# Emitting the stores, squares and splits of finished residual blocks three row pairs later

## The chip, the cores and the metric

The kernel runs on one core of one Trainium2 chip. The metric is the device time of one execution in microseconds (us). The kernel before takes 2199.36 us, the median of three runs (2192.54 to 2201.11). All work of the core goes through five engines: TensorE (PE, matmuls into PSUM), VectorE (DVE), ScalarE (ACT), GpSimd (POOL), and SyncE (SP), which here issues every DMA.

## The reference, cut to what matters

The model has two layers over one sequence of 1024 tokens of width 1024. Layer 0 is an RG-LRU block, layer 1 a chunked band attention whose keys and values are computed once from the residual stream after layer 0. Each layer ends in the same MLP:

```
def sqrelu_mlp(x, w_up, w_down):
    return jnp.square(jax.nn.relu(x @ w_up)) @ w_down

for l in range(DEPTH):                      # DEPTH = 2
    h = h + recurrent_block(...)            # l = 0
    h = h + o @ b_w_o[j]                    # l = 1, after attention
    h = h + sqrelu_mlp(rmsnorm(h, mlp_norm[l]), w_up[l], w_down[l])
```

The hidden width is 4096. The change is in the product with `w_down` and in what follows it: the finished residual block of layer 0 is stored (attention adds to it later), squared (for the next RMS norm) and split (as an operand of the next projections); that of layer 1 is the output and is stored only.

## The kernel before, in words

**Numbers.** Activations are held transposed: 128 features on the partitions, half of the tokens (512 columns, `h` 0 or 1) in a tile. Every float32 product is done as three matmuls on fp32r operands (`mm`, lines 321 to 323): high part by high part, low weight by high part, and so on. So each weight block and each activation block has first to be split: ACT copies it to the high part, DVE subtracts that from the source to get the low part (`wsplit`, lines 732 and 733, for weights; `split`, lines 334 and 335, for activations).

**The down product.** `mlp_down` (line 805) is one level of a fast 2 by 2 block multiplication: instead of eight half-size products it does seven, in the order n = 0, 1, 5, 4, 6, 2, 3. Each product runs over 16 row pairs q of the hidden dimension. For a row pair, `block(n, q)` gets one weight block (loaded from HBM, or kept from an earlier product and added to), and splits it; `operand(n, q)` loads one activation block from the scratch tensor `hid` and splits it; then 12 matmuls (four PSUM banks, three each) use both. Products 0, 5, 6 and 3 accumulate in the banks `Z` (tags pj and sc), products 1, 4 and 2 in `Y` (tags tp and po), so that neighbours always use different banks.

**After a product**, `add` (line 851) adds the four banks to residual blocks `X[j][h]`, four DVE instructions. After products 1, 6 and 2 four blocks are complete, and `finish(j0, h)` (line 853) calls `done` for each. In layer 0 `done1` (line 912) stores the block to `x2d`, and `o2.last` squares it on ACT (line 368), adds the square to a running sum on DVE (line 374; not for the first block of a half, which begins the sum) and splits it (lines 334, 335). In layer 1 `done2` (line 1324) only stores it to the output. After product 3, the last one, the last four blocks are finished one by one.

**Buffers.** Landing buffers `raw`: 8. Pool `w` (16 tiles): split weights, and the split operands of products 0, 1, 5 and 4. Pool `g` (66 tiles): the residual blocks, weight sums kept between products, the running sum of squares, the split finished blocks, and the split operands of products 6, 2 and 3 (line 846: `where=gr if n in (6, 2, 3) else wr`). A row pair takes two tiles for the weight and two for the operand.

**What sets the order.** In this stage the order of instructions on an engine isn't written out by hand. A scheduler of the framework orders them when the program is built, on a model of the times, with the program's order as priority, and it hands out the tiles of the pools. Each engine then runs its list in order. (Attention is different: there the order is that in which the kernel's own planner emits it.) After product 2, `ahead()` (layer 0 only, `begin_later`, line 307) begins to load and prepare the weights of the attention stage.

Of the kernel before, what the change touches and what calls it, by code (L numbers as in the profile page):

```python
# [36 lines left out]
FR = 0.9  # L37
LAT = 0.3
C_DMA = 3.8
JP = 2  # L40
SC = (2.5, 5.0)
AHEAD = 1
# [111 lines left out]
def tile_yoco_rglru_chunk_attention(  # L154
# [30 lines left out]
    def nm(s):  # L185
        cnt[0] += 1
        return f"{s}_{cnt[0]}"

    def gf(s="g"):
        return gp.tile([P, H2], F32, tag="g", name=nm(s))  # L190
# [7 lines left out]
    def rawf():  # L198
        return wp.tile([P, H2], F32, tag="raw", name=nm("raw"), bufs=NRAW)
# [10 lines left out]
    def bank(tag=None):  # L210
        if tag is None:
            tag = ("pj", "tp", "sc", "pj", "tp", "sc", "po", "sc")[ring[0] % 8]
            ring[0] += 1
        return ps1.tile([P, H2], F32, tag=tag, name=nm(tag), bufs=BANKS[tag])

    def hs(h):
        return slice(h * H2, (h + 1) * H2)
# [3 lines left out]
    def dma(dst, src):  # L221
        ins = nc.sync.dma_start(dst, src)
        if early[0]:
            early[0] -= 1
            tc.keep_in_program_order(ins)
# [28 lines left out]
    for t in range(NF):  # L254
        later += [(w_kv[t], g_kv, pool), (w_q[t], g_q, pool), (w_kv[NF + t], g_kv, pool)]
    later += [(w_o[j], None, WOE) for j in range(JP)]
    later.append((w_o[:, :, NF - 1, :].rearrange("j p m -> p j m"), None, dve))
    later += [(w_o[j], None, dve) for j in range(JP, NF)]
    loading, ready = [], []
# [58 lines left out]
    def mm(ps, wp_, xp, start, stop, more=False):  # L318

        (wh, wl), (xh, xl) = wp_, xp  # L320
        pe.matmul(ps, lhsT=wh, rhs=xh, start=start, stop=False, skip_group_check=more)  # L321
        pe.matmul(ps, lhsT=wh, rhs=xl, start=False, stop=False, skip_group_check=more)  # L322
        pe.matmul(ps, lhsT=wl, rhs=xh, start=False, stop=stop, skip_group_check=more)  # L323

    def mm3(ps, w, xs, half, span=None):
        n = len(xs)
        for k in range(n) if span is None else span:
            mm(ps, wparts(w, k), xs[k][half], k == 0, k == n - 1)

    def split(src, gain=None, where=gr):  # L330
        h = where("h")
        l = where("l")
        if gain is None:
            act.activation(h, src, AF.Copy)  # L334
            dve.tensor_tensor(l, src, h.bitcast(F32), ALU.subtract)  # L335
        else:
            act.activation(h, src, AF.Copy, scale=gain)
            dve.scalar_tensor_tensor(l, src, gain, h.bitcast(F32), ALU.mult, ALU.subtract)  # L338
        return h, l
# [319 lines left out]
    class Out:  # L659
# [54 lines left out]

        def whole(self, Z, j0):
            ws = {}
            for j, h in out_order(j0):
                if j not in ws:
                    ws[j] = next_w()
                ps = bank()  # L720
                mm3(ps, ws[j], Z, h)
                self.first(ps, j, h)
                self.last(j, h)

    def wload(src):
        raw = rawf()
        dma(raw, src)
        return raw

    def wsplit(raw):  # L730
        wh, wl = wr("wh"), wr("wl")
        act.activation(wh, raw, AF.Copy)  # L732
        dve.tensor_tensor(wl, raw, wh.bitcast(F32), ALU.subtract)  # L733
        return blocks4(wh), blocks4(wl)
# [70 lines left out]
    def mlp_down(o, layer, done, ahead=None):  # L805
        X = [[gf("x") for _ in range(2)] for _ in range(NF)]
        S = [None] * NQ
        S2 = [None] * NQ

        def block(n, q):  # L810

            def load(x):
                return wload(w_down[layer, q, x])

            if n == 0:
                a11, a21 = load(A11), gf("s3")
                dma(a21, w_down[layer, q, A21])
                w = wsplit(a11)
                dve.tensor_tensor(a21, a21, a11, ALU.add)
                S[q] = a21  # L820
            elif n == 1:
                a12, a22 = load(A12), gf("s2")
                dma(a22, w_down[layer, q, A22])
                w = wsplit(a12)
                dve.tensor_tensor(a22, a22, S[q], ALU.add)
                S2[q] = a22
            elif n == 5:
                w = wsplit(S2[q])
                a12 = load(A12)
                dve.tensor_tensor(S2[q], S2[q], a12, ALU.add)  # L830
            elif n == 4:
                a21, a22 = load(A21), load(A22)
                dve.tensor_tensor(a21, a21, a22, ALU.add)
                w = wsplit(a21)
            elif n == 6:
                w = wsplit(S[q])
            elif n == 2:
                w = wsplit(S2[q])
            else:
                w = wsplit(load(A22))  # L840
            return w

        def operand(n, q):
            t = rawf()
            dma(t, hid[n, q])
            return split(t, where=gr if n in (6, 2, 3) else wr)

        def add(banks, j0, h, op):
            for x in range(4):
                xt = X[j0 + x][h]  # L850
                dve.tensor_tensor(xt, xt, banks[x], op)

        def finish(j0, h):
            for x in range(4):
                done(j0 + x, h, X[j0 + x][h])

        Z = [bank(tag) for tag in ("pj", "pj", "sc", "sc")]
        for n in (0, 1, 5, 4, 6, 2, 3):
            if n in (1, 4):
                Y = [bank(tag) for tag in ("tp", "tp", "tp", "po")]  # L860
            banks = Y if n in (1, 4, 2) else Z
            start = n in (0, 1, 4)
            held = []
            for q in range(NQ):
                held.append((block(n, q), operand(n, q)))
                if n == 0 and q < NF:
                    for h in range(2):
                        dma(X[q][h], o.keep[q, :, hs(h)])
                if n == 3 and NQ - 4 <= q < NQ - 1:
                    continue  # L870
                for x in range(4):
                    for p, ((wh, wl), t) in enumerate(held):
                        mm(
                            banks[x], (wh[:, x, :], wl[:, x, :]), t,
                            start and q == 0, q == NQ - 1 and p == len(held) - 1, not start,
                        )
                held = []
            if n == 0:
                add(Z, 0, 0, ALU.add)
            elif n == 1:  # L880
                add(Y, 0, 0, ALU.add)
                finish(0, 0)
            elif n == 5:
                add(Z, 0, 1, ALU.add)
            elif n == 4:
                add(Y, 4, 1, ALU.subtract)
            elif n == 6:
                add(Z, 4, 1, ALU.subtract)
                finish(4, 1)
            elif n == 2:  # L890
                add(Y, 0, 1, ALU.add)
                finish(0, 1)
                if ahead is not None:
                    ahead()
            else:
                for x in range(4):
                    xt = X[4 + x][0]
                    dve.tensor_tensor(xt, xt, Z[x], ALU.subtract)
                    done(4 + x, 0, xt)
# [16 lines left out]

    mlp_up(o1, 0)
    mlp_down(o1, 0, done1, begin_later)


# [13 lines left out]
    class Proj:  # L934
# [35 lines left out]
        def normed(self, kind, h, ps):  # L970
# [51 lines left out]
            for e, st in enumerate((even, odd)):  # L1022
                (self.K if keys else self.Q)[e][h] = st
            self.made[kind, h].set(plan.t + C_DMA)

# [51 lines left out]
    def load_bias(hd):  # L1077
        b = biases[hd] = sf(640)
        dma(b, relb[hd])
        yield plan.t + C_DMA  # L1080
        pool.tensor_scalar(b, b, -1.0, 1.0, ALU.mult, ALU.mult)
# [4 lines left out]
    class Unit:  # L1086
# [142 lines left out]
        def reload(self, k, h):  # L1229
            ot = sf()  # L1230
            dma(ot, od[k, :, hs(h)])
            yield plan.t + C_DMA
            yield from self.halves(k, h, ot, REL)
# [13 lines left out]
    def wo_steps():  # L1247
        for j0 in range(0, JP, 2):
            js = range(j0, min(j0 + 2, JP))
            ws = []  # L1250
# [17 lines left out]
    def filling():  # L1268
        for t in range(NF):
            projs.append(Proj(t))  # L1270
            n = 0
            for y in projs[t].steps():
                if y is None:
                    n += 1
                    if t == NF - 1 and 0 <= n - 5 * NF - 2 < NF - 2:
                        plan.start(units[0].reload(n - 5 * NF - 2, 0))
                yield y
        yield from wo_steps()

    fill = filling()  # L1280
    total = 8 * 6 * NF + 2 * JP * (NF - 1)
    cost = [1.0 if n.h else FR for n in units]
# [31 lines left out]
    wl7 = next_w()  # L1314
    for j in range(JP):
        for h in range(2):
# [71 lines left out]
```

## Time and profile before

| what | us |
|---|---|
| median of three runs | 2199.36 |
| profiled execution, its own time | 2197.24 |
| its span, first to last instruction | 2195.5 |
| TensorE busy in it | 2113.9 |
| VectorE busy | 1583.7 |
| ScalarE busy | 1115.1 |
| down products of layer 0, about | 655.9 to 985.2 |
| down products of layer 1, about | 1878.7 to 2191.3 |

The profile is one execution. Times in it run from its first instruction. Busy time of matmuls overlaps (each is shown 0.39 us long, but the next one starts 0.23 us after it), so progress of PE is read here from the starts of matmuls, and a loss from a start that comes later than the one before it allows.

### The profile page before, as it was taken

Reading aid. Unit: us, or ns where it says so; the run is one execution under the profiler, and the core shown is the slowest. Engines: PE = TensorE matmul, PEld = TensorE weight load, DVE = VectorE, ACT = ScalarE, POOL = GpSimd, SP = SyncE. Lnnn points to the kernel's source line nnn. Section 1 sums busy time; section 2 is a strip of 40 time slices with the busy share of each in tenths; the row PEclk is TensorE's granted clock in tenths of the full one; section 3 lists DMA queues with packets and bytes.
Section 4 is the critical chain, followed back from the end, with each engine's and each line's share of the span. In section 5 each row is a group of like instructions: output and inputs, shape, how many; then the busy total and the mean of one; then the engine's idle time right before and its main releaser. Section 6 shows DMA issues by size and latency. Waiting matters only on the chain.

```text
span 2195.5 us, 29616 instructions
## 1 busy us (share of the span) xinstructions
PE 2113.9 (96%) x9753; PEld 1741.9 (79%) x9753; DVE 1583.7 (72%) x2716; ACT 1115.1 (51%) x2030; POOL 659.8 (30%) x567
## 2 busy tenths in 40 slices
PE   7898898999999999998999999999999999999999
PEld 5676686888888888776888888878788888888887
DVE  7788867777777775554777777777677777777843
ACT  4576745443444544444666666675443443444632
POOL 5454311333320000105666656651223333000000
PEclk8999999999999999999999999999999999999999
DMA  5111144444459774343333333353354444977733
GB/s 178 37 48 37 37 141 134 163 149 149 154 196 328 241 257 134 125 144 94 90 85 87 80 80 88 92 174 111 97 184 156 152 146 153 336 262 240 255 103 99
DMA packets 176746, 319.21 MB, mean 145 GB/s; under 512 B 20816, under 2 KB 23120, under 8 KB 176592
## 3 DMA queue, kind: packets, MB, share of 16 engines
q1 hardware_dynamic: 176592, 317.33, 44.6%
q8 instruction: 76, 1.25, 0.2%
q14 instruction: 78, 0.64, 0.1%
HBM read 219.73 MB, written 78.64 MB: 136 GB/s over the span
## 4 chain that ended last, share of the span: by engine, by line
PE 77%; DVE 11%; DMA 4%; issue 3%; ACT 3%; POOL 2%; SPq 1%; DVEq 0%; POOLq 0%; ACTq 0%
PE pj L321 11%; PE pj L322 11%; PE pj L323 11%; PE tp L322 6%; PE tp L321 6%; PE tp L323 6%; PE sc L321 4%; PE sc L322 4%; PE sc L323 4%; PE tp L1172 2%; DVE c L577 2%; PE po L1200 1%; DVE l L335 1%; DMA s<-in_xT 1%; PE po L1199 1%
## 5 line engine op out<-in xcount | busy, mean ns | idle before, releaser
L321 PE MATMUL pj<-h,wh 128*128 128x512 f32 x1269 | 509.9, 402 | 8.9 <-ACT h L334 4.4
L322 PE MATMUL pj<-l,wh 128*128 128x512 f32 x1269 | 497.4, 392 | 2.9 <-DVE l L338 2.0
L323 PE MATMUL pj<-h,wl 128*128 128x512 f32 x1269 | 496.7, 392 | 0.0
L732 ACT ACTIVATE wh<-raw 128x512 fp32r<-128x512 f32 x352 | 221.6, 630 | 339.0 <-PE po L322 81.4
L733 DVE TENSOR_TENSOR wl<-raw,wh 128x512 fp32r<-128x512 f32 x352 | 277.0, 787 | 116.6 <-ACT wh L732 113.2
L321 PEld LDWEIGHTS pj<-h,wh 128*128 128x128 f32 x1269 | 239.9, 189 | 56.0 <-ACT h L334 4.9
L323 PEld LDWEIGHTS pj<-h,wl 128*128 128x128 f32 x1269 | 239.4, 189 | 51.4
L322 PEld LDWEIGHTS pj<-l,wh 128*128 128x128 f32 x1269 | 240.3, 189 | 45.8 <-DVE l L338 2.9
L321 PE MATMUL tp<-h,wh 128*128 128x512 f32 x657 | 258.4, 394 | 5.0 <-ACT h L334 4.4
L322 PE MATMUL tp<-l,wh 128*128 128x512 f32 x657 | 258.4, 393 | 2.9 <-DVE l L335 2.8
L323 PE MATMUL tp<-h,wl 128*128 128x512 f32 x657 | 257.8, 392 | 0.0
L321 PE MATMUL sc<-h,wh 128*128 128x512 f32 x569 | 224.6, 395 | 6.8 <-DVE rec L556 6.8
L322 PE MATMUL sc<-l,wh 128*128 128x512 f32 x569 | 223.9, 393 | 3.0 <-DVE l L335 3.0
L323 PE MATMUL sc<-h,wl 128*128 128x512 f32 x569 | 223.6, 393 | 0.0
L765 POOL TENSOR_TENSOR raw<-raw,raw 128x512 f32<-128x512 f32 x32 | 52.2, 1631 | 396.1 <-DVE wl L733 374.9
L335 DVE TENSOR_TENSOR l<-raw,h 128x512 fp32r<-128x512 f32 x224 | 153.2, 694 | 22.2 <-ACT h L334 20.8
L747 ACT ACTIVATE s<-s 128x512 f32<-128x512 f32 x128 | 80.3, 629 | 170.1 <-DVE s L746 170.1
L334 ACT ACTIVATE h<-raw 128x512 fp32r<-128x512 f32 x224 | 136.6, 620 | 52.9 <-DMA raw<-hid 30.9
L321 PEld LDWEIGHTS tp<-h,wh 128*128 128x128 f32 x657 | 124.7, 190 | 32.2 <-ACT h L334 5.2
L322 PEld LDWEIGHTS tp<-l,wh 128*128 128x128 f32 x657 | 124.8, 190 | 31.1 <-DVE l L335 4.8
L287 POOL TENSOR_TENSOR wl<-raw,wh 128x512 fp32r<-128x512 f32 x74 | 105.6, 1433 | 134.2 <-ACT wh L284 133.4
L323 PEld LDWEIGHTS tp<-h,wl 128*128 128x128 f32 x657 | 124.7, 190 | 26.6 <-DVE wl L733 0.6
(262 smaller groups left out, 3971.0 us busy)
## 6 DMA issues: line engine op xcount, KB each, us to landing
hid<-s SPq DMA_DIRECT2D x224, 256.0 KB, 2.0
raw<-hid SPq DMA_DIRECT2D x224, 256.0 KB, 3.7
raw<-in_w_down SPq DMA_DIRECT2D x192, 256.0 KB, 3.5
raw<-in_w_up SPq DMA_DIRECT2D x128, 256.0 KB, 2.6
s<-in_w_down SPq DMA_DIRECT2D x64, 256.0 KB, 4.4
raw<-in_w_kv SPq DMA_DIRECT2D x32, 256.0 KB, 3.5
raw<-in_w_in SPq DMA_DIRECT2D x31, 256.0 KB, 3.1
od<-ev SPq DMA_DIRECT2D x48, 128.0 KB, 2.3
```

The costliest lines, as they stand in the source:

```text
L287: eng.tensor_tensor(wl, raw, wh.bitcast(F32), ALU.subtract)
L321: pe.matmul(ps, lhsT=wh, rhs=xh, start=start, stop=False, skip_group_check=more)
L322: pe.matmul(ps, lhsT=wh, rhs=xl, start=False, stop=False, skip_group_check=more)
L323: pe.matmul(ps, lhsT=wl, rhs=xh, start=False, stop=stop, skip_group_check=more)
L334: act.activation(h, src, AF.Copy)
L335: dve.tensor_tensor(l, src, h.bitcast(F32), ALU.subtract)
L577: dve.scalar_tensor_tensor(ct, rec[h][:, k : k + H2], vec[:, V_CW + k, n : n + 1], ct, ALU.mult, ALU.add)
L732: act.activation(wh, raw, AF.Copy)
L733: dve.tensor_tensor(wl, raw, wh.bitcast(F32), ALU.subtract)
L747: act.activation(out, out, AF.Square)
L765: pool.tensor_tensor(raw[A11], raw[A11], raw[A21], ALU.add)
L1172: pe.transpose(pt[:, g * P : (g + 1) * P], sc[:, (kb - kb0) * P : (kb - kb0 + 1) * P], ident)
```

## The change

The call of `finish` after products 1, 6 and 2 is put off into the next product: it is noted in a list, and emitted in row pair 3 of that product, after the weight block and the operand of that row pair, before its matmuls. `add` stays where it was, and so does what follows product 3. It holds for both layers, which share the function.

```
+DEFER = 3
...
+        left = []
         for n in (0, 1, 5, 4, 6, 2, 3):
...
             for q in range(NQ):
                 held.append((block(n, q), operand(n, q)))
+                if q == DEFER:
+                    for j0, h in left:
+                        finish(j0, h)
+                    left = []
...
             elif n == 1:
                 add(Y, 0, 0, ALU.add)
-                finish(0, 0)
+                left.append((0, 0))
...
             elif n == 6:
                 add(Z, 4, 1, ALU.subtract)
-                finish(4, 1)
+                left.append((4, 1))
             elif n == 2:
                 add(Y, 0, 1, ALU.add)
-                finish(0, 1)
+                left.append((0, 1))
                 if ahead is not None:
                     ahead()
```

So finish(0, 0) moves into product 5, finish(4, 1) into product 2, finish(0, 1) into product 3, and there behind `ahead()`. No instruction is added or removed.

## Rows read from the trace of the kernel before

**Rows 1.** The page: busy time, share of the span, instructions of each engine.

```profile
PE 2113.9 (96%) x9753; PEld 1741.9 (79%) x9753; DVE 1583.7 (72%) x2716; ACT 1115.1 (51%) x2030; POOL 659.8 (30%) x567
```

**Rows 2.** Waits of PE from 650 to 1000: total us, times, longest.

```profile
PE tp L321 <- ACT h L334: 4.4, 1, 4.4
PE pj L321 <- ACT h L334: 4.4, 1, 4.4
PE pj L322 <- DVE l L335: 0.8, 1, 0.8
```

**Rows 3.** Timeline of PE, layer 0, product 6 to 2: start, length, instruction, [idle before].

```profile
882.17 0.39 PE L323 MATMUL sc<-h,wl 128*128 128x512 f32 x1
887.00 1.65 PE L321 MATMUL tp<-h,wh 128*128 128x512 f32 x3 [4.44 <-ACT h L334]
...
892.45 0.63 PE L323 MATMUL po<-h,wl 128*128 128x512 f32 x1
892.88 0.49 PE L321 MATMUL tp<-h,wh 128*128 128x512 f32 x1
```

**Rows 4.** Timeline of PE, layer 0, product 2 to 3, and the last of 3.

```profile
933.60 0.39 PE L323 MATMUL po<-h,wl 128*128 128x512 f32 x1
938.43 1.22 PE L321 MATMUL pj<-h,wh 128*128 128x512 f32 x2 [4.44 <-ACT h L334]
...
985.24 0.39 PE L323 MATMUL sc<-h,wl 128*128 128x512 f32 x1
```

**Rows 5.** Timeline of PE, layer 1: last matmuls of products 6, 2 and 3.

```profile
2104.23 0.39 PE L323 MATMUL sc<-h,wl 128*128 128x512 f32 x1
...
2147.75 0.39 PE L323 MATMUL po<-h,wl 128*128 128x512 f32 x1
...
2191.27 0.39 PE L323 MATMUL sc<-h,wl 128*128 128x512 f32 x1
```

**Rows 6.** Stretches of layer 0: length, busy time of engines, granted clock (PEclk), DMA.

```profile
870.00:880.00 10.00, 10.00 (x46) 8.29 (x45) 2.21 (x4) 2.25 (x4) 0.00 (x0) 1.00 0.01 2
885.00:890.00 5.00, 2.78 (x6) 1.77 (x7) 5.00 (x10) 5.00 (x11) 0.00 (x0) 0.62 0.09 25
```

**Rows 7.** Timelines of ACT, layer 0, products 6 to 2.

```profile
879.65 0.63 ACT L732 ACTIVATE wh<-s 128x512 fp32r<-128x512 f32 x1 [2.09 <-PE sc L322]
881.64 0.63 ACT L368 ACTIVATE acc<-x 128x512 f32<-128x512 f32 x1 [1.36 <-DVE x L851]
...
885.81 0.61 ACT L334 ACTIVATE h<-x 128x512 fp32r<-128x512 f32 x1
886.33 4.25 ACT L334 ACTIVATE h<-raw 128x512 fp32r<-128x512 f32 x8
```

**Rows 8.** Timeline of SP's queue, the same boundary.

```profile
881.63 2.11 SPq L222 DMA_DIRECT2D x2d<-x  x4
888.84 4.54 SPq L222 DMA_DIRECT2D raw<-hid  x8
```

**Rows 9.** Timeline of ACT and SP's queue, layer 1, products 6 to 2.

```profile
2099.53 0.62 ACT L334 ACTIVATE h<-raw 128x512 fp32r<-128x512 f32 x1
...
2103.70 2.12 SPq L222 DMA_DIRECT2D out<-x  x4
```

**Rows 10.** Timeline of DVE, layer 0: adds and finish between products 6 and 2.

```profile
880.92 1.28 DVE L851 TENSOR_TENSOR x<-x,pj 128x512 f32<-128x512 f32 x2
...
887.53 0.69 DVE L733 TENSOR_TENSOR wl<-s,wh 128x512 fp32r<-128x512 f32 x1
888.13 4.90 DVE L335 TENSOR_TENSOR l<-raw,h 128x512 fp32r<-128x512 f32 x8
```

**Rows 11.** Timeline of DVE, layer 0: finish between products 2 and 3.

```profile
934.75 0.69 DVE L374 TENSOR_TENSOR acc<-acc,s 128x512 f32<-128x512 f32 x1
939.56 0.69 DVE L733 TENSOR_TENSOR wl<-raw,wh 128x512 fp32r<-128x512 f32 x1
```

**Rows 12.** Timeline of PE, then DVE, layer 0: end of 1 and of 5; finish.

```profile
751.34 0.39 PE L323 MATMUL po<-h,wl 128*128 128x512 f32 x1
...
795.13 0.39 PE L323 MATMUL sc<-h,wl 128*128 128x512 f32 x1
...
752.49 0.69 DVE L335 TENSOR_TENSOR l<-x,h 128x512 fp32r<-128x512 f32 x1
756.70 0.68 DVE L830 TENSOR_TENSOR s<-s,raw 128x512 f32<-128x512 f32 x1
757.30 0.69 DVE L335 TENSOR_TENSOR l<-raw,h 128x512 fp32r<-128x512 f32 x1
```

More of the change, by code (lines that the diff above doesn't have):

```diff
@@ L39 @@
 C_DMA = 3.8
+DEFER = 3
 JP = 2
@@ L857, in mlp_down @@
         Z = [bank(tag) for tag in ("pj", "pj", "sc", "sc")]
+        left = []
         for n in (0, 1, 5, 4, 6, 2, 3):
@@ L865, in mlp_down @@
                 held.append((block(n, q), operand(n, q)))
+                if q == DEFER:
+                    for j0, h in left:
+                        finish(j0, h)
+                    left = []
                 if n == 0 and q < NF:
@@ L881, in mlp_down @@
                 add(Y, 0, 0, ALU.add)
-                finish(0, 0)
+                left.append((0, 0))
             elif n == 5:
@@ L888, in mlp_down @@
                 add(Z, 4, 1, ALU.subtract)
-                finish(4, 1)
+                left.append((4, 1))
             elif n == 2:
                 add(Y, 0, 1, ALU.add)
-                finish(0, 1)
+                left.append((0, 1))
                 if ahead is not None:
```

## The prediction

> **What bounds the kernel now.** I read the page first: TensorE is busy 2113.9 us of 2195.5, no other engine above 72% [rows 1]. So time can be won only where PE stands still or runs slowly. The waits of PE over the down products of layer 0 name two large ones: 4.4 us each, once on bank tp and once on pj, both for the high part of an operand split (L334), and one of 0.8 us for a low part [rows 2]. The timeline of PE places them: the first between the last matmul of product 6 and the first of product 2, the second between products 2 and 3 [rows 3, 4]. The granted clock beside them is 1.00 before the gap and 0.62 on average from 885 to 890 [rows 6]: PE comes back at the lower level (1.2 instead of 2.4 GHz), and the reader sees it in the starts, 0.43 us apart at 892.45 and 892.88 instead of 0.227.
>
> So the loss is larger than the waits, and I take it from whole products, against the same products of layer 1. From the last matmul of one product to that of the next are 192 matmuls. Layer 1 needs 2147.75 - 2104.23 = 43.52 us for product 2 and 2191.27 - 2147.75 = 43.52 for product 3 [rows 5]; that is 0.2267 us a matmul or 2.72 us a row pair. Layer 0 needs 933.60 - 882.17 = 51.43 and 985.24 - 933.60 = 51.64 [rows 3, 4]. The losses are 7.91 and 8.12 us. Product 5, the third one that follows a finish, takes 795.13 - 751.34 = 43.79, a loss of 0.27 [rows 12].
>
> **Why PE stands still.** Between 879.65 and 881.64 ACT is idle, and eight operand blocks for product 2 lie in the landing buffers: it splits eight in a row from 886.33, and only after these do new loads of hid start, at 888.84 [rows 7, 8]. Yet the first of them is behind the last split of the finished blocks (885.81), which waits for the add, which waits for the end of product 6. In layer 1, with the same product and no finished blocks to split, the operand splits go on before the end of product 6 (2099.53 against 2104.23) [rows 9], and PE never waits. The difference isn't room: in the last row pairs of product 6 the pool g holds 16 residual blocks, 16 kept weight sums, 8 split blocks and one sum of squares, and a few operands; more than 20 of its 66 tiles are free, and the trace then fills 1 + 8 + 16 = 25 of them in one go (rows 7: a sum, four split blocks, eight operands). I read it so: tiles of a pool are handed out in program order, and the eight tiles for the split finished blocks stand ahead of the operands of the next product. After product 1 the operands are in pool w, where nothing of finish stands ahead of them, and there the loss is 0.27. Three boundaries, and each behaves as this reading says.
>
> **The change part by part.** In layer 0 the three calls of finish hold 12 stores, 12 squares and 12 splits: on ACT 8 instructions a call, 0.52 us apart; on DVE 7, 7 and 8, 0.60 us apart (752.49 to 756.70 is seven, 934.75 to 939.56 eight [rows 11, 12]).
>
> Products 2 and 3: the operands of row pairs 0 to 3 now stand ahead of finish in the order of pool g. Their eight tiles are free well before the end of the product before, and the blocks are loaded. So PE goes on without a pause, at the full clock, for four row pairs, 10.9 us. What is late next is row pair 4, which now stands behind finish. PE needs it at 882.17 + 0.23 + 10.88 = 893.3 in product 2 and at 933.60 + 0.23 + 10.88 = 944.7 in product 3. DVE: the adds start at 880.92 as before, four of them and seven of finish end at 887.5 [rows 10]; three weight splits that fall due meanwhile make 1.8, the low part of row pair 4 another 0.7: 890.0, 3.3 us early. In product 3: finish ends at 939.6 [rows 11], plus 1.8 and 0.7 is 942.1, 2.6 us early. Afterwards a row pair costs DVE two instructions, 1.2 of 2.72 us, and it catches up. Gain 7.91 + 8.12 = 16.03 us. The bounds: nothing, if the pause only moves to row pair 4, and no more than the 16.03, since PE then runs like layer 1.
>
> Product 5: here finish only changes places on DVE. Before, it stands ahead of the low part for row pair 2 (757.30 [rows 12]), and PE loses 0.27. After: adds end at 752.5, five instructions for row pairs 2 and 3 at 755.5, seven of finish at 759.7, the weight and operand of row pair 4 at 761.0; PE needs them at 751.34 + 0.23 + 10.88 = 762.5, 1.5 us in hand. So 0.27 is gained. Bounds: 0.27 gained, to 4.2 lost if all seven instructions of finish push row pair 4 (its cover, 1.5 us, gone and no slack found); I take the gain, because the order of the queue decides and the same instructions fit.
>
> SP's queue: the four stores of a call, 2.11 us of issue [rows 8], now stand behind the loads of the operands of row pairs 0 to 3. They hold nothing that is needed early, and the landing buffers hold eight blocks of advance; layer 1 issues its four stores, 2.12 us, among loads without a wait of PE [rows 9]. Cost nothing; if that cover went, at most 2.1 us a call. The weight loads and preparation that ahead() starts now stand ahead of the third finish on SP, ACT and POOL; POOL has nothing of finish. In the rows of the kernel before they run during product 2, where ACT and DVE have most of their time free (2.25 and 2.21 of 10 us at 870 to 880 [rows 6], and the same afterwards). Cost nothing; at worst one split, 0.5 us.
>
> Layer 1: the calls hold only stores, take no tiles, and PE has no pause there to win. Zero, within 2.1 us either way for stores that meet loads.
>
> Sum: 16.03 + 0.27 = 16.3 us. What follows layer 0 hangs on the last matmul of product 3 and moves with it. The profiled execution took 2197.24 us, 1.7 more than its span: 2197.2 - 16.3 = 2180.9. It lies 2.1 below the median of the runs; against that median 2199.4 - 16.3 = 2183.1. I forecast **2183**.
>
> **A rule that speaks against it.** At 881.64 to 886.33 ACT runs what stands first in its list although blocks behind it are ready [rows 7]. The Trainium skill (Perfetto Trace Analysis, Tensor Engine Instruction) says of ACT and DVE that they are strict first in, first out, so a put-off group still holds up all that stands behind it: by that alone the pause would move to row pair 4 rather than go, and the sum would be nothing. The trace agrees on the order; what the rule leaves out is the four row pairs that PE then has in hand.
>
> **The rivals.** (1) Half: one of the two pauses stays, for the scheduler may place the splits of product 3 otherwise (there a row pair has two loads, and five operands instead of eight lay ready). Then about 8 us are won: 2191. For it: margins of 2.6 us are worked out from one order only. Against: both pauses have one cause and one size. (2) The change does not do what it says, because the scheduler puts the operands after finish all the same, say since free tiles and not their order decide. Then 2199. Against: over 20 free tiles, and layer 1. (3) Slower: finish lands as one burst on DVE before row pair 4, and the scheduler, which now takes it for less urgent, holds it until PE is at row pair 3; operands behind it in pool g wait for it. Then the pause of about 8 us moves from row pair 0 to row pair 4 in products 2 and 3, which gains nothing, and product 5, which had cover, pays one such pause too: 2199 + 8 = 2207. It decides from the point where finish ends later than 893.3 - 0.7, that is 5 us later than now. Against: ACT is busy 2.25 of 10 us at the end of product 6 [rows 6], so a list built from such times has room for finish as soon as the add is done.
>
> **How the numbers follow.** The forecast gets 0.71, half 0.13, nothing 0.10, slower 0.06. The forecast's own range is the lowest and highest run less 16.3, 2176 to 2185, and up to 2188 for a residue of a few us. To leave out no more than 2 in 10 the range goes to the half case with its scatter: 2176 to 2194. A difference under 0.5% (11 us) can't be told from none with this scatter; the border is at 2188.4. Faster by more: nearly all of the forecast and a tenth of the rest, 0.74; within: 0.20; slower: 0.06.
>
> **What would show it.** In the changed kernel's timeline ACT splits at least four operands (h<-raw) before the last matmul of products 6 and 2 of layer 0; PE shows no pause there, the granted clock stays at 1.00, and both products take 43.5 us. Product 5 takes 43.5. If PE waits at row pair 4, rival 3 or the rule holds; if at row pair 0, rival 2. The forecast is wrong, too, if both products take 43.5 us and the total doesn't follow, that is if something after layer 0 gives the 16 us back.

## The result, and the profile after

The kernel after takes 2182.56 us, the median of four runs (2181.75 to 2183.55), against 2200.03 for the kernel before beside it (2192.54 to 2201.11). The ratio is 0.9928, with a 95% interval of 0.9906 to 0.9951: faster by 0.5 to 0.9%, or 11 to 21 us. The forecast was 2183, 16.3 us less than before.

The profiled execution's span is 2180.9 us, 14.6 less than before. Line numbers of the kernel after are one higher up to the loop of the products (L334 is now L335, L851 is L852).

First the waits of PE from 650 to 1000 in the kernel after, the whole answer; it stands against [rows 2].

```profile
PE pj L322 <- DVE s L782: 0.7, 1, 0.7
```

Both waits of 4.4 us are gone, and that of 0.8 us; what is left belongs to the up product (L782), which has a wait of 0.4 us before, too (L781, not among the three lines of [rows 2]). Now the timeline of PE in the kernel after, as in [rows 3, 4, 12]: the last matmuls of products 1, 5, 6, 2 and 3 of layer 0, and the first of product 2. Columns: start, length, instruction.

```profile
752.42 0.39 PE L324 MATMUL po<-h,wl 128*128 128x512 f32 x1
...
795.95 0.39 PE L324 MATMUL sc<-h,wl 128*128 128x512 f32 x1
...
882.99 0.39 PE L324 MATMUL sc<-h,wl 128*128 128x512 f32 x1
883.21 0.39 PE L322 MATMUL tp<-h,wh 128*128 128x512 f32 x1
...
926.50 0.39 PE L324 MATMUL po<-h,wl 128*128 128x512 f32 x1
...
970.02 0.39 PE L324 MATMUL sc<-h,wl 128*128 128x512 f32 x1
```

Product 2 follows product 6 after 0.22 us, where it took 4.83. The differences of the starts give the products:

| layer 0 | before, us | after, us |
|---|---|---|
| product 5 | 43.79 | 43.53 |
| product 2 | 51.43 | 43.51 |
| product 3 | 51.64 | 43.52 |

From the end of product 1 to that of product 3 the kernel before needs 985.24 - 751.34 = 233.90, the kernel after 970.02 - 752.42 = 217.60: 16.30 less. The stretch view (length, busy time of PE, PEld, DVE, ACT and POOL, granted clock, share and GB/s of DMA) shows the clock that fell to 0.62 in [rows 6]:

```profile
885.00:890.00 5.00, 5.00 (x23) 4.13 (x22) 5.00 (x9) 4.86 (x10) 0.00 (x0) 1.00 0.21 78
```

The timeline of ACT in the kernel after says why; it answers to [rows 7].

```profile
857.38 0.64 ACT L335 ACTIVATE h<-raw 128x512 fp32r<-128x512 f32 x1 [0.24 <-DVE wl L734]
...
880.46 0.63 ACT L733 ACTIVATE wh<-s 128x512 fp32r<-128x512 f32 x1 [2.09 <-PE sc L323]
882.45 0.63 ACT L369 ACTIVATE acc<-x 128x512 f32<-128x512 f32 x1 [1.35 <-DVE x L852]
...
886.64 0.62 ACT L335 ACTIVATE h<-x 128x512 fp32r<-128x512 f32 x1
887.16 0.62 ACT L335 ACTIVATE h<-raw 128x512 fp32r<-128x512 f32 x1
```

The fourth operand split of product 2 is at 857.38, 25 us before product 6 ends. Then come weight splits alone, then finish from 882.45 to 886.64, and right behind it row pair 4. The reader should compare the place of finish with before: its first square starts 0.54 us ahead of the last matmul's start (882.45 against 882.99), and before 0.53 (881.64 against 882.17). So finish, emitted three row pairs later in the program, does not run later. What moved are the operands of four row pairs, which now run ahead of it.

### The profile page after: what moved, and what is told of

It is laid out like the page before. It is cut to its first block, busy times and chain, and to the rows that moved or that the text cites. A ratio compares the mean times of both kernels' runs of the same rounds, so it can differ in the third digit from the quotient of the medians.

```text
span 2180.9 us, 29620 instructions
## 1 busy us (share of the span) xinstructions
PE 2112.1 (97%) x9753; PEld 1742.7 (80%) x9753; DVE 1579.6 (72%) x2716; ACT 1114.8 (51%) x2030; POOL 661.4 (30%) x567
## 4 chain that ended last, share of the span: by engine, by line
PE 78%; DVE 10%; DMA 4%; ACT 3%; issue 3%; POOL 2%; SPq 0%; DVEq 0%; ACTq 0%; POOLq 0%
PE pj L322 12%; PE pj L324 11%; PE pj L323 11%; PE tp L323 6%; PE tp L322 6%; PE tp L324 6%; PE sc L322 5%; PE sc L323 5%; PE sc L324 4%; PE tp L1178 2%; DVE c L578 2%; PE po L1206 1%; DMA s<-in_xT 1%; PE po L1205 1%; PE sc L1153 1%
## 5 line engine op out<-in xcount | busy, mean ns | idle before, releaser
L335 ACT ACTIVATE h<-raw 128x512 fp32r<-128x512 f32 x224 | 137.2, 620 | 56.8 <-DMA raw<-hid 33.1
```

## The experiments

Theory A is that of the prediction: tiles of pool g go out in program order, so that the operands of the next product can't be split before the tiles that stand ahead of them are in use; a pause remains as far as too few row pairs are in hand. Every kernel below is the kernel after with one edit. Each time stands beside runs of the kernel before on the same chip: median 2197.48 in the first four, 2197.81 in the others. Products are from one profiled execution of each, as above.

**How far to put off: 0, 1, 8, 14 instead of 3**

```
-DEFER = 3
+DEFER = 0        # e2: 1, e3: 8, e4: 14
```

> Only change against the kernel after: the put-off group is emitted in row pair 0 instead of 3, so one row pair of operands stands ahead of it in pool g. Theory A (cover: tiles of pool g go out in program order, and PE has one row pair of 2.72 us in hand for each operand that stands ahead of finish): without cover the first low part reached PE 6.7 us after the last matmul of product 6, so one row pair of cover leaves about 3 us of loss in products 2 and 3 each at the full clock, up to 5 if the granted clock falls: 2189 to 2193 in all. Theory B (it is enough that finish no longer stands between two products): 2183, no pause.

Measured: 2190.21 us (2188.38 to 2191.64), ratio 0.9967 (0.9957 to 0.9977). Products 5, 2 and 3 take 43.82, 48.03 and 49.88, so products 2 and 3 lose 4.5 and 6.4 us. The total fits, but product 3 loses more than the 5 us that were expected at most. The timeline of PE in this kernel, after the first row pair of product 2 (the bracket holds the idle time and what ended it):

```profile
884.79 0.39 PE L324 MATMUL po<-h,wl 128*128 128x512 f32 x1
886.91 0.96 PE L322 MATMUL tp<-h,wh 128*128 128x512 f32 x3 [1.73 <-ACT h L335]
887.71 0.40 PE L322 MATMUL po<-h,wh 128*128 128x512 f32 x1
888.77 0.80 PE L323 MATMUL tp<-l,wh 128*128 128x512 f32 x1 [0.67 <-DVE l L336]
889.37 0.63 PE L324 MATMUL tp<-h,wl 128*128 128x512 f32 x1
889.80 0.63 PE L323 MATMUL tp<-l,wh 128*128 128x512 f32 x1
```

Product 6 ended at 882.07; the 12 matmuls of one row pair run, then PE waits as before, 2.7 us less. The low part arrives 6.70 us after the last matmul of product 6 (888.77 - 882.07), as it did in the kernel before (888.87 - 882.17). That is what theory A asks for; theory B, which held it to be enough that finish leaves the gap between two products, is wrong.

> The put-off group in row pair 1, two row pairs of cover, 5.4 us. Theory A: a pause of under 1 us before row pair 2 of products 2 and 3 of layer 0, without a fall of the granted clock: 2184 to 2185. Theory B: 2183, no pause.

Measured: 2183.56 us (2178.99 to 2183.68), ratio 0.9932 (0.9909 to 0.9954). Products 5, 2 and 3 take 43.82, 43.82 and 44.38. One wait is named, before the low parts of row pair 2 of product 3, at the full granted clock; the pause that was expected in product 2 is too short to be named, 0.3 us in all. First PE, then the stretch:

```profile
936.27 0.50 PE L323 MATMUL pj<-l,wh 128*128 128x512 f32 x1 [0.57 <-DVE l L336]
```

```profile
935.00:940.00 5.00, 4.43 (x20) 3.35 (x19) 4.50 (x9) 2.10 (x4) 0.00 (x0) 1.00 0.62 166
```

In the total the 1.5 us that the three products lose are not told from nothing; in the trace they are plain.

> The put-off group in row pair 8. Theory A: cover beyond 6.7 us buys nothing, so 2183 as with 3. Rival (a later group comes as a burst that collides with a busier DVE or with fewer operands in hand): each of the three products loses up to 8 us, 2191 to 2207.

Measured: 2183.30 us (2179.63 to 2184.27), ratio 0.9935 (0.9916 to 0.9953). Products 5, 2 and 3 take 43.52 each, and PE doesn't wait once between 700 and 1000.

> The put-off group in row pair 14, with one operand of the product behind it and the next finish close. Theory A: still 2183, since the group runs while PE has operands in hand; at most 2 us more at the end of product 3, where the last four blocks are finished too. Rival of the burst: 2191 to 2207, with pauses of PE in the last row pairs of products 5, 2 and 3.

Measured: 2182.70 us (2179.62 to 2183.35), ratio 0.9932 (0.9914 to 0.9950). Products 5, 2 and 3 take 43.52 each, no wait.

So the gain is flat from two row pairs or so upwards, as theory A has it. After product 6, finish doesn't come late in either of the two. In the timeline of ACT with 14 its first square still starts as soon as the add allows (the last matmul of product 6 is at 882.68):

```profile
882.21 0.63 ACT L369 ACTIVATE acc<-x 128x512 f32<-128x512 f32 x1 [1.42 <-DVE x L852]
```

After product 2 with 14 a part of it does. The squares (s, whose tiles come from another pool) run at once. The splits of the same blocks, which take tiles of pool g, run 20 us behind the last matmul of product 2 (926.20), right after the fifteenth operand split of product 3 (h<-raw):

```profile
925.67 1.23 ACT L369 ACTIVATE s<-x 128x512 f32<-128x512 f32 x2
...
927.32 1.14 ACT L369 ACTIVATE s<-x 128x512 f32<-128x512 f32 x2
...
945.61 0.63 ACT L335 ACTIVATE h<-raw 128x512 fp32r<-128x512 f32 x1 [0.92 <-DMA raw<-hid]
946.15 1.14 ACT L335 ACTIVATE h<-x 128x512 fp32r<-128x512 f32 x2
...
948.75 0.62 ACT L335 ACTIVATE h<-raw 128x512 fp32r<-128x512 f32 x1
```

With 8 they start 3.5 us behind it, after the ninth operand (927.61 against 924.09). PE doesn't wait for either: with 14 one operand stands behind these splits, split at 948.75 and needed at 967.2 (926.20 + 0.23 + 15 row pairs). What a late finish costs when PE soon needs what stands behind it, the rival of the burst, is not tested by this.

The same order shows in every kernel. A product has 16 operand splits; counted in their order on ACT, as many of them run ahead of the first split of a finished block as the program emits ahead of it:

| | before | 0 (e1) | 1 (e2) | 3 (after) | 8 (e3) | 14 (e4) |
|---|---|---|---|---|---|---|
| row pairs emitted ahead of finish | 0 | 1 | 2 | 4 | 9 | 15 |
| operand splits ahead of it, product 2 | 0 | 1 | 2 | 4 | 9 | 15 |
| operand splits ahead of it, product 3 | 0 | 1 | 2 | 4 | 9 | 15 |

In product 5, whose operands come from pool w, it is 3 in all of them. With 14, eleven operands more than with 3 are split before product 6 ends, which is 22 tiles of pool g: so tiles were free and ACT had the time, and the order held the operands back. So, as far as these kernels show, the place in the program is a priority and an order of tiles: what takes no tile of pool g runs when it is ready, and what takes one waits for its turn.

**Which part of finish: squares or splits**

The edit is cut; the comments tell which half is called at once.

```
+    def square1(j, h, x):
+        dma(x2d[j, :, hs(h)], x)
+        o2.XR[j][h] = x
+        o2.norm.add(h, x)
+
+    def split1(j, h, x):
+        o2.XS[j][h] = split(x)
...
                 add(Z, 4, 1, ALU.subtract)
+                # layer 0, e5: square1 for the four blocks here, split1 put off
+                # layer 0, e6: split1 here, square1 put off
                 left.append((4, 1))
```

> In layer 0 stores and squares stay right after the add, as before; only the splits of the finished blocks are put off to row pair 3. Theory A (order of the tiles of pool g): between products 2 and 3 nothing of pool g stands ahead of the operands, so no pause at all; between 6 and 2 only one tile does, that of the new sum of squares, so operands start one square after the add (882.2 instead of 886.3) and PE loses 1 to 2 us: 2184 to 2186. Rival C (the pause is the time that ACT and DVE need for finish, half of which stays): half of each pause stays, 2191.

Measured: 2182.49 us (2181.49 to 2185.09), ratio 0.9931 (0.9916 to 0.9945). Products 2 and 3 take 45.04 and 43.51. ACT in this kernel at the end of product 6 (last matmul at 880.83):

```profile
880.29 0.63 ACT L369 ACTIVATE acc<-x 128x512 f32<-128x512 f32 x1 [1.36 <-DVE x L852]
880.83 0.62 ACT L335 ACTIVATE h<-raw 128x512 fp32r<-128x512 f32 x1
881.35 1.66 ACT L369 ACTIVATE s<-x 128x512 f32<-128x512 f32 x3
```

The square that takes a tile of pool g (acc) holds the first operand; the moment it has started, the operand follows, ahead of the other squares. After product 2, where no square takes such a tile, there is no pause. The 1.5 us of product 2 were expected and are there; the total, expected at 2184 to 2186, doesn't show them.

> The mirror: in layer 0 the splits of finished blocks stay right after the add; stores and squares are put off to row pair 3. Theory A: eight tiles of pool g stand ahead of the operands as before, so both pauses stay nearly whole, 6 to 8 us each: 2195 to 2200. Rival C: half of each pause goes, 2191.

Measured: 2195.46 us (2192.71 to 2197.69), ratio 0.9986 (0.9977 to 0.9995). Products 2 and 3 take 50.10 and 50.88, a loss of 6.6 and 7.4. PE at the two boundaries:

```profile
885.99 0.50 PE L322 MATMUL tp<-h,wh 128*128 128x512 f32 x1 [4.00 <-ACT h L335]
...
936.54 1.22 PE L322 MATMUL pj<-h,wh 128*128 128x512 f32 x2 [4.44 <-ACT h L335]
```

In the program half of the work is put off, and nearly all of the pause stays; the other half is put off in the experiment before, and nearly all of the pause goes. Rival C asked for 2191 in both. This kernel alone doesn't part order from time, since after product 6 three of the four squares run on ACT all the same, between the splits and ahead of the first operand (885.33). The kernel with the squares left in place does, and so does the kernel after: its finish takes ACT from 882.45 to 887.26, as long as before (881.64 to 886.42), and PE doesn't wait. So it is the tiles of the splits, not the time that ACT and DVE spend on finish. The counts above fit here, too: 4 operands ahead of the finished splits in both products where the splits are put off, none where they stay.

**One boundary, one layer**

```
             elif n == 1:
                 add(Y, 0, 0, ALU.add)
-                left.append((0, 0))
+                finish(0, 0)
...
-                left.append((0, 1))
+                finish(0, 1)
```

> Only the finish after product 6 is put off, the other two stay. Theory A: product 2 takes 43.5 us, product 3 keeps its 8.1 us of loss: 2191 to 2192, so the two gains add up. Rival (one pause feeds the other, or the gain of one is given back in the next product): about 2183 or about 2199.

Measured: 2189.91 us (2187.55 to 2192.40), ratio 0.9963 (0.9948 to 0.9977). Products 5, 2 and 3 take 43.79, 43.52 and 52.21, with 4 and no operand splits ahead of finish in products 2 and 3. The total is 1.1 us under the expected 2191 to 2192; against the kernel before beside it, it is 7.9 us less, one boundary's worth. The gain of one boundary is there alone, and the other keeps its pause:

```profile
932.61 0.96 PE L322 MATMUL pj<-h,wh 128*128 128x512 f32 x2 [4.44 <-ACT h L335]
```

> Only the stores of layer 1 are put off, layer 0 as before. Theory A: no tiles and no pause there, so nothing: 2199 to 2200, PE starts in products 5, 2 and 3 of layer 1 as before. Rival (the stores hold up loads on SP's queue): 2 us or more gained, 2197 or below.

In layer 0 finish is called at once, in layer 1 it is put off. Measured: 2197.34 us (2194.62 to 2200.73), ratio 0.9997 (0.9987 to 1.0006). The median is under the expected 2199 to 2200, but so is that of the kernel before beside it, by which the difference is 0.5 us; the interval, 2.9 us less to 1.3 more, doesn't by itself rule out the rival's 2 us. The trace does: products 5, 2 and 3 of layer 1 take 43.52 each, products 2 and 3 as in [rows 5]. Products 2 and 3 of layer 0 take 50.23 and 52.61.

No experiment points to a version better than the kernel after: it already has no wait in the three products, and 8, 14 and the squares left in place come out within 1 us of it.

## Why the prediction was right

**The loss and where it sits.** Named from whole products of layer 0 against those of layer 1, 7.91 + 8.12 + 0.27. After: 43.51, 43.52 and 43.53 instead of 51.43, 51.64 and 43.79, that is 7.92, 8.12 and 0.26. The e7 kernel shows that the boundaries are independent.

**The cause.** Predicted from three boundaries: tiles of pool g in program order. Shown by the counts, which are those of the program's order at both boundaries in every kernel; by the kernel with 14, where squares and splits of the same blocks are emitted in one place and only the splits wait, behind fifteen operands; by the pair e5 and e6, where the pause follows the splits; and by the single acc tile, which holds up one operand split for the length of one square. The strict order of ACT's list, weighed against the change, is broken in none of the rows shown here; but it doesn't say what stands in the list. The operands were behind finish because the list was made so, and the change remade the list. One reading was loose: ACT is idle from 880.28 to 881.64, since its instruction of 879.65 takes 0.63 us.

**What is late next.** Row pair 4 was to come 3.3, 2.6 and 1.5 us early in products 2, 3 and 5. The low parts end at 889.6, 933.8 and 762.1, and PE needs them 11.11 us (0.23 and four row pairs) after the last matmul of the product before (882.99, 926.50, 752.42): 4.5, 3.9 and 1.4 us early. In products 2 and 3 the three weight splits that I put ahead of it come partly behind it. From DVE in the kernel after, the last instruction of finish and the next ones, product 2 (first fence) and product 3:

```profile
887.74 0.68 DVE L336 TENSOR_TENSOR l<-x,h 128x512 fp32r<-128x512 f32 x1
888.34 0.68 DVE L734 TENSOR_TENSOR wl<-s,wh 128x512 fp32r<-128x512 f32 x1
888.94 0.68 DVE L336 TENSOR_TENSOR l<-raw,h 128x512 fp32r<-128x512 f32 x1
```

```profile
931.87 0.68 DVE L336 TENSOR_TENSOR l<-x,h 128x512 fp32r<-128x512 f32 x1
932.47 0.68 DVE L734 TENSOR_TENSOR wl<-raw,wh 128x512 fp32r<-128x512 f32 x1
933.07 0.68 DVE L336 TENSOR_TENSOR l<-raw,h 128x512 fp32r<-128x512 f32 x1
```

**Costs put at nothing.** The stores behind other loads, the weights of the attention stage ahead of the third finish, layer 1: PE has no wait in the products concerned of either layer, and e8 gives a ratio of 0.9997 for layer 1 alone.

**The rivals.** Half, nothing and slower did not happen. Half is what e7 builds, 2189.91 where 2191 was worked out for it. The slower one needs a finish that runs late with operands behind it that PE soon needs. The late splits in product 3 with 14 had a single operand behind them, so the price was not put to the test.

**The rest of the way.** 16.30 us are won in layer 0, and the span is 14.6 shorter. The kernel after was 1.08 us later at the end of product 1 (752.42 against 751.34), where the two have done the same work, and needs 1210.9 instead of 1210.3 us after product 3. Over the ten profiled executions the first figure lies between 750.0 and 754.5 and the second between 1208.1 and 1210.9, so both lie within the scatter of single executions, and nothing shows that something was given back. By the medians 17.5 us are won. That the total lies within 0.5 us of the forecast is partly luck, as the runs of the kernel before alone spread over 8.6 us; the gains of the three products, right to 0.01 us, are not.

## What to carry to other kernels

Where a scheduler hands out the tiles of a pool in program order, a finished result that takes a long-lived tile from the pool of the next stage's operands keeps that stage from running ahead, even with tiles free and ACT idle (22 tiles more were filled in time when only the order changed): look for an engine that idles with its input loaded, then for what stands ahead of it in the pool. The runs show one remedy: emit the result behind as many of the next operands as cover its time (here 6.7 us, two to three row pairs of 2.72). Put off far, its splits come late in turn (20 us with 14); nothing here needed them sooner. Another is only suggested: give the two different pools, as product 5 has them (its loss was 0.27; a pool of its own for the finished splits in products 2 and 3 was not tried). And take a pause of PE from whole stages, because the clock afterwards costs as well.

## What the runs showed of the hardware that was not expected

The granted clock did not fall after every pause. In e2 and e5 PE stood still for up to 0.6 us at a time and stayed at 1.00 (e5, 880 to 885, in the first fence). In e1, waits of 1.73 and 0.67 us with four matmuls between them were followed by matmuls 0.43 us apart, the lower of the two levels (1.2 GHz), against 0.227 at the upper (2.4 GHz). Products 2 and 3 of e1 lost 4.5 and 6.4 us. Their waits add up to 2.4 and 3.0 us (1.73 each for the high part, 0.67 and 1.26 for the low part), so what is lost beyond the waits, 2.1 and 3.4 us, differs more than the waits do. In product 2 six starts in a row come 0.43 us after the one before, in product 3 twelve; at 0.2 us each that is 1.2 and 2.4 us of it. The granted clock in a stretch of e5, then in five us after each wait of e1 (the other columns as above):

```profile
880.00:885.00 5.00, 4.08 (x17) 2.74 (x16) 5.00 (x9) 4.71 (x9) 0.00 (x0) 1.00 0.69 236
```

```profile
890.00:895.00 5.00, 5.00 (x19) 4.01 (x19) 3.23 (x6) 2.77 (x6) 0.00 (x0) 0.79 0.64 194
...
940.00:945.00 5.00, 5.00 (x16) 3.92 (x16) 2.72 (x4) 2.16 (x5) 0.00 (x0) 0.67 0.95 317
```
